# Loading-queue transfers for the block rows, late decays and h; roots on GpSimd; PSUM copies on ScalarE

## The chip, the cores and the metric

The kernel runs on one core of a Trainium2 chip. The metric is the device time of one execution in microseconds. The engines are named as the profile names them: PE is TensorE's matmul side, DVE is VectorE, ACT is ScalarE, POOL is GpSimd and SP is the engine whose queue issues the weight loads ("the loading queue").

## What is computed

One decoder block on 256 tokens of width 2048, in float32: a gated feed-forward layer, a mixer of two kinds of heads, a second feed-forward layer, gated per-layer embeddings and a final norm.

```python
def block(x, p, ...):                      # one block, SEQ = 256 tokens, D_MODEL = 2048, float32
    h = x
    h = h + 0.5 * swiglu(rmsnorm(h, ffn1_norm), w_gate, w_up, w_down)
    proj = rmsnorm(h, mix_norm) @ w_in
    g_qkv, g_gate, g_a, g_b, s_z, s_xbc, s_dt = jnp.split(proj, IN_SPLITS, axis=-1)
    o_gdn = gdn_mixer(g_qkv, g_gate, g_a, g_b, ...)       # 8 gated delta heads of 128
    o_ssm = ssd_mixer(s_z, s_xbc, s_dt, ...)              # 16 state-space heads of 64, 2 groups
    h = h + jnp.concatenate([o_gdn, o_ssm], axis=-1) @ w_out
    h = h + 0.5 * swiglu(rmsnorm(h, ffn2_norm), ...)
    gate = jax.nn.sigmoid(rmsnorm(h, ple_norm) @ ple_w_gate)
    h = h + gate * rmsnorm(p @ ple_w_proj, ple_post_norm)
    return rmsnorm(h, final_norm)

def gdn_mixer(qkv, gate, a, bl, conv_w, a_log, dt_bias, norm_w):
    qkv = jax.nn.silu(causal_depthwise_conv(qkv, conv_w))
    q, k, v = jnp.split(qkv, 3, axis=-1)                  # per head:
    q = l2norm(q) * 128 ** -0.5                           # x * rsqrt(sum(x * x) + EPS)
    k = l2norm(k)
    beta = jax.nn.sigmoid(bl)
    g = -jnp.exp(a_log) * jax.nn.softplus(a + dt_bias)
    o = gated_delta_rule_chunked(q, k, v, g, beta)        # a triangular solve per head and chunk
    return rmsnorm(o, norm_w) * jax.nn.silu(gate)
```

The state-space heads (`ssd_mixer`) are built alike: a causal convolution, decays from exponentials of cumulated sums, products per chunk and a state that is passed on.

## The kernel before

The work runs in stages. The positions are those of the profiled execution. The first feed-forward layer takes 0 to 764 us, the mixer 764 to 1156, the output projection `wout` 1156 to 1260, the second feed-forward layer 1260 to 2012, and the embeddings with the final norm the rest.

**Weights.** Tiles `raw` of 1 MB (128 x 2048) are loaded by SP (`load`, L108 to L112) into three buffers. Each is split in two pieces of 1024 columns: ScalarE casts the piece to a rounded format, `hi` (L119), and VectorE subtracts to get the rest, `lo` (L120); four buffers of each exist. In the mixer `single` (L136 to L150) multiplies a tile: for each of 16 blocks of 128 columns three matmuls, L146, L147 and L148, 48 in a tile and 24 in a piece. These are called weight matmuls below. A `lo` split needs the buffer that an earlier piece leaves when its last matmul is done.

**The mixer.** The projection by `w_in` goes on tile after tile, and the small work of the heads is interleaved with it. `delta_rule(i)` projects q, k and v of two delta heads (a pair, four of them) and starts the generator `gdn_pair`; `state_space(i)` does so for four state-space heads (a quad, four of them) with `ssd_quad`. A generator runs one piece further at each `tick()` of the weight loop, so its code order is tied to the weight loop. The scheduler then orders each engine's instructions on a simulated timeline and by priority, and each engine runs its list strictly in order.

The steps of a pair, with their lines:

1. `kk` (L578): products of k with k and q in a PSUM bank. L583 to L591 form `LA`, the decayed triangular blocks, and `ss`, the sums of squares.
2. `rs` (L602): the root `1/sqrt` of eight sums by `rsq` (L208 to L218), 11 VectorE steps: two integer steps for a first guess and three Newton steps of three. `irk` (L603) and `rq` (L605) follow from it.
3. Four small DMAs on GpSimd's queue write the 32-wide diagonal blocks of `LA` to DRAM as `blkl` (L612), and one reads them back as `Lb` (L614), each repeated over partitions, 512 KB. `Z` is preset to the unit blocks (L618), `Y` to zero (L621).
4. `xv` (L629) and `kd` (L636): ScalarE scales the transposed v and k.
5. The elimination: 31 columns of two VectorE steps each, `tb` (L645) and `Z` (L647), which invert the diagonal blocks.
6. `Z` goes to DRAM as `blky` (L648) and comes back in four parts as `Y` (L653), all on GpSimd's queue. VectorE transposes `Y` into `oT` (L656).
7. Two levels of small products, `ip`, `ix` and `iy` (L667), extend the inverse from blocks of 32 to 128.
8. The chain over the two chunks: `y0` (PSUM copy L703), `st` (copy to `S`, L707), `o0`, `ks` and `qs` (L711 to L716), `y1` (copy L719), `o1` (L722).
9. The output norm: squares on ScalarE (L727), `rq2` (L729 to L731), the root `ro` (L732) and its product with `rq` (L733), the scaling of `o` on ScalarE (L735), a transpose on TensorE, `ot` (L740), and a copy to `oT` (L741).

**Quads and decays.** The rows of cumulated decays lie in DRAM; `spread` (L427) reads them back onto all partitions into the space of `hT`, whose content is parked in DRAM as `hold` and read back at the end of the mixer (L873). `decay` adds a mask on GpSimd (L435) and takes exponentials on ScalarE (L439); `er` (L451) holds further ones. `late_decay` (L474) does this for quads 2 and 3 after the space is free. In `ssd_quad` two products of 128 x 512 on VectorE multiply the decays by `CB` (L802).

**Other roots.** `stats` (L220 to L239) uses the same `rsq` for the norms between stages; `finalrow` belongs to the final one.

The functions that the diff touches:

## Time and profile before

| what | us |
|---|---|
| median of 3 runs | 2114.48 |
| lowest and highest of them | 2114.13, 2115.96 |
| the profiled execution, its own time | 2113.53 |
| its span, first to last instruction | 2111.7 |
| PE busy in the span | 2069.7 |
| DVE busy | 1385.1 |
| ACT busy | 1030.4 |
| POOL busy | 130.8 |
| mean granted TensorE clock | 0.991 of full |

PE is busy 98% of the span. The view of stages gives the busy time of each engine between two positions, so a pause of PE is the length of the stretch less its busy time. The timelines list single instructions; in square brackets stands how long the engine had been idle before, and whose end released it. An `x4` in a row joins four instructions of one kind.

### The profile page before, as it was taken

What the parts mean: (1) busy time and instruction counts of PE and PEld (TensorE: products, weight loads), DVE (VectorE), ACT (ScalarE), POOL (GpSimd) and SP (SyncE); (2) the same over time, 40 slices, a digit from 0 to 9 for tenths busy, and PEclk for the clock granted to TensorE, in tenths of its full rate; (3) what the DMA queues carried; (4) which work ended last, traced back from release to release, by engine and by line L of the source; (5) the groups of instructions that cost most, each with busy time, mean ns of one, the idle gap of its engine ahead of it and who ended that gap; (6) DMA issues with size and microseconds to landing.
All of it is one profiled execution on the core that took longest, in us unless ns stands there. A gap on an engine that the chain in (4) does not pass through costs nothing.

```text
span 2111.7 us, 31624 instructions
## 1 busy us (share of the span) xinstructions
PE 2069.7 (98%) x12880; PEld 1848.4 (88%) x12880; DVE 1385.1 (66%) x2251; ACT 1030.4 (49%) x1529; POOL 130.8 (6%) x139
## 2 busy tenths in 40 slices
PE   8999999999999999999799999999999999999997
PEld 7888888888888899998798998888888888888886
DVE  7665555556556768989787667665555555556685
ACT  6444444444444556644344546544444444445553
POOL 2000000000000113001120011000000000000010
PEclk9999999999999999999899999999999999999998
DMA  7555455655545665553433545555456555545652
GB/s 252 192 184 183 171 180 190 213 180 187 192 165 188 208 209 187 195 208 124 144 133 140 184 163 198 193 187 182 165 189 206 196 181 184 195 157 185 207 189 100
DMA packets 63937, 384.58 MB, mean 182 GB/s; under 512 B 7584, under 2 KB 8864, under 8 KB 30640
## 3 DMA queue, kind: packets, MB, share of 16 engines
q1 hardware_dynamic: 59904, 372.04, 51.1%
q0 software_dynamic: 3888, 10.52, 1.8%
q8 instruction: 101, 1.65, 0.3%
q14 instruction: 44, 0.36, 0.1%
HBM read 377.78 MB, written 4.75 MB: 181 GB/s over the span
## 4 chain that ended last, share of the span: by engine, by line
PE 96%; DVE 2%; DMA 1%; issue 0%; ACT 0%; SPq 0%; POOL 0%; DVEq 0%; POOLq 0%
PE mm L131 49%; PE mm L129 24%; PE mm L147 6%; PE mm L148 6%; PE mm L146 6%; PE mm L133 1%; DVE lo L120 0%; DMA hT<-in_xT 0%; PE ip L667 0%; PE pj L131 0%; DMA blky<-Z 0%; PE py L814 0%; PE iy L667 0%; PE kk L578 0%; DVE pp L972 0%
## 5 line engine op out<-in xcount | busy, mean ns | idle before, releaser
L120 DVE TENSOR_TENSOR lo<-raw,hi 128x1024 fp32r<-128x1024 f32 (+1 forms) x774 | 858.6, 1117 | 487.3 <-ACT hi L119 486.5
L131 PE MATMUL mm<-xs,hi 128*128 128x512 f32 x3088 | 1079.2, 398 | 1.9 <-ACT hi L119 1.9
L119 ACT CAST hi<-raw 128x1024 fp32r<-128x1024 f32 (+1 forms) x774 | 744.5, 962 | 626.6 <-PE mm L131 374.9
L129 PE MATMUL mm<-xs,lo 128*128 128x256 f32 x2895 | 813.8, 281 | 3.4 <-DVE lo L120 3.4
L131 PEld LDWEIGHTS mm<-xs,hi 128*128 128x128 f32 x3088 | 568.8, 188 | 127.6 <-ACT hi L119 2.7
L129 PEld LDWEIGHTS mm<-xs,lo 128*128 128x128 f32 x2895 | 547.4, 189 | 13.4 <-DVE lo L120 5.0
L131 PE MATMUL mm<-hid,hi 128*128 128x512 f32 x1408 | 492.5, 397 | 0.0
L129 PE MATMUL mm<-hid,lo 128*128 128x256 f32 x1344 | 377.8, 281 | 0.0
L131 PEld LDWEIGHTS mm<-hid,hi 128*128 128x128 f32 x1408 | 260.2, 188 | 59.1
L129 PEld LDWEIGHTS mm<-hid,lo 128*128 128x128 f32 x1344 | 253.3, 188 | 3.0
L148 PE MATMUL mm<-xs,lo 128*128 128x256 f32 x816 | 232.9, 285 | 1.4 <-DVE lo L120 1.4
L146 PE MATMUL mm<-xs,hi 128*128 128x256 f32 x816 | 233.1, 286 | 0.0
L147 PE MATMUL mm<-xs,hi 128*128 128x256 f32 x816 | 232.4, 285 | 0.0
L148 PEld LDWEIGHTS mm<-xs,lo 128*128 128x128 f32 x816 | 156.5, 192 | 1.9 <-DVE lo L120 1.8
L146 PEld LDWEIGHTS mm<-xs,hi 128*128 128x128 f32 x816 | 156.7, 192 | 0.6 <-DVE cin L364 0.4
L147 PEld LDWEIGHTS mm<-xs,hi 128*128 128x128 f32 x816 | 156.6, 192 | 0.4 <-issue 0.2
L169 ACT COPY t<-mm 128x256 f32<-128x256 f32 x167 | 62.2, 373 | 160.1 <-PE mm L131 159.1
L170 DVE TENSOR_TENSOR t<-t,mm 128x256 f32<-128x256 f32 x167 | 69.8, 419 | 85.6 <-ACT t L169 85.5
L206 POOL TENSOR_TENSOR acc<-acc,sq 128x512 f32<-128x512 f32 x43 | 64.9, 1509 | 956.4 <-ACT sq L205 956.4
L169 ACT COPY s<-mm 128x256 f32<-128x256 f32 x88 | 32.7, 372 | 149.9 <-PE mm L131 149.9
L170 DVE TENSOR_TENSOR s<-s,mm 128x256 f32<-128x256 f32 x88 | 37.1, 421 | 74.2 <-ACT s L169 74.2
L146 PE MATMUL mm<-osp,hi 128*128 128x256 f32 x256 | 72.6, 284 | 1.2 <-ACT osp L196 1.2
(305 smaller groups left out, 1432.3 us busy)
## 6 DMA issues: line engine op xcount, KB each, us to landing
raw<-in_wgu SPq DMA_DIRECT2D x173, 1024.0 KB, 4.8
raw<-in_wd SPq DMA_DIRECT2D x128, 704.0 KB, 4.1
raw<-in_win SPq DMA_DIRECT2D x52, 1024.0 KB, 4.8
raw<-in_wout SPq DMA_DIRECT2D x16, 1024.0 KB, 4.8
raw<-in_wple SPq DMA_DIRECT2D x16, 1024.0 KB, 4.8
first<-in_wgu SPq DMA_DIRECT2D x12, 256.0 KB, 7.2
hold<-hT POOLq DMA_DIRECT2D x4, 512.0 KB, 3.9
hT<-rows POOLq DMA_DIRECT2D x4, 512.0 KB, 9.6
```

Of the source, the lines that this page charges most:

```text
L119: act.copy(hi, src)
L120: dve.tensor_tensor(out=lo, in0=src, in1=hi.bitcast(F32), op=ALU.subtract)
L129: pe.matmul(ps[:, 0, :], lo[:, w, :], act_in[:, k, 0, :], start=False, stop=False, skip_group_check=True)
L131: pe.matmul(ps, hi[:, w, :], act_in[:, k], start=start, stop=stop, skip_group_check=True)
L133: pe.matmul(ps[:, 0, :], lo[:, w, :], act_in[:, k, 0, :], start=False, stop=False, skip_group_check=True)
L146: pe.matmul(ps[:, 0, :], hi[:, i, :], act_in[:, k, 0, :], start=k == ks[0], stop=False)
L147: pe.matmul(ps[:, 0, :], hi[:, i, :], act_in[:, k, 1, :], start=False, stop=False)
L148: pe.matmul(ps[:, 0, :], lo[:, i, :], act_in[:, k, 0, :], start=False, stop=k == ks[-1])
L169: act.copy(out, ps[:, 0, :])
L170: dve.tensor_tensor(out=out, in0=out, in1=ps[:, 1, :], op=ALU.add)
L206: pool.tensor_tensor(out=acc, in0=acc, in1=sq, op=ALU.add)
```

## The change

- `rsq` takes its first value from GpSimd's power function and makes one Newton step of three VectorE steps after it. `stats` uses it.
- `rsq_aside` is new: the same wholly on GpSimd, the power and four steps. `rs` and `ro` use it. `irk`, `rq`, `rq2` and the product of `ro` and `rq` move from VectorE to GpSimd. A constant tile `mhalf` holds the exponent.
- The transfers `Lb`, the rows of `late_decay` and the reload of `hold` are issued by SP rather than GpSimd.
- The preset of `Z` moves from GpSimd to VectorE, and behind the four yields ahead of the elimination.
- The PSUM copies `y0`, `S` and `y1` move from VectorE to ScalarE, the products with `CB` from VectorE to GpSimd.

A line of the new kernel is that of before less 1 up to `rsq`, and plus 11 from about L219 on.

```diff
@@ -9,7 +9,6 @@
 
 F32 = mybir.dt.float32
 F32R = mybir.dt.float32r
-I32 = mybir.dt.int32
 AF = mybir.ActivationFunctionType
 ALU = mybir.AluOpType
 PSUM = bass.MemoryType.PSUM
@@ -208,14 +207,26 @@
     def rsq(m, n, name):
 
         y = small.tile([P, n], F32, tag=f"rsq{n}", name=name)
+        pool.tensor_tensor(out=y, in0=m, in1=mhalf[:, :n], op=ALU.pow)
         t = small.tile([P, n], F32, tag=f"rsqt{n}", name=name + "t")
-        dve.tensor_scalar(t.bitcast(I32), m.bitcast(I32), 1, None, op0=ALU.logical_shift_right)
-        dve.tensor_scalar(y.bitcast(I32), t.bitcast(I32), -1.0, float(0x5F3759DF), op0=ALU.mult, op1=ALU.add)
-        for _ in range(3):
-            dve.tensor_tensor(out=t, in0=y, in1=y, op=ALU.mult)
-            dve.scalar_tensor_tensor(out=t, in0=t, scalar=-0.5, in1=m, op0=ALU.mult, op1=ALU.mult)
-            dve.scalar_tensor_tensor(out=y, in0=t, scalar=1.5, in1=y, op0=ALU.add, op1=ALU.mult)
+        dve.tensor_tensor(out=t, in0=y, in1=y, op=ALU.mult)
+        dve.scalar_tensor_tensor(out=t, in0=t, scalar=-0.5, in1=m, op0=ALU.mult, op1=ALU.mult)
+        dve.scalar_tensor_tensor(out=y, in0=t, scalar=1.5, in1=y, op0=ALU.add, op1=ALU.mult)
         return y
+
+    def rsq_aside(m, n, name):
+
+        y = small.tile([P, n], F32, tag=f"rsq{n}", name=name)
+        pool.tensor_tensor(out=y, in0=m, in1=mhalf[:, :n], op=ALU.pow)
+        t = small.tile([P, n], F32, tag=f"rsqt{n}", name=name + "t")
+        pool.tensor_tensor(out=t, in0=y, in1=y, op=ALU.mult)
+        pool.tensor_tensor(out=t, in0=t, in1=m, op=ALU.mult)
+        pool.tensor_scalar(t, t, -0.5, 1.5, op0=ALU.mult, op1=ALU.add)
+        pool.tensor_tensor(out=y, in0=t, in1=y, op=ALU.mult)
+        return y
+
+    mhalf = cp.tile([P, 16], F32, name="mhalf")
+    pool.memset(mhalf, -0.5)
 
     def stats(squares, width, name, use, wait=2):
 
@@ -424,9 +435,9 @@
 
         ers = {}
 
-        def spread(d, src):
-
-            nc.gpsimd.dma_start(d, src.unsqueeze(0).to_broadcast([P, *src.shape]))
+        def spread(d, src, queue=nc.gpsimd):
+
+            queue.dma_start(d, src.unsqueeze(0).to_broadcast([P, *src.shape]))
 
         def decay(d, h0, n):
 
@@ -472,7 +483,7 @@
                 yield from quad_decay(i)
 
         def late_decay(i):
-            spread(quad_dec(i), rows[:, 8 + 4 * i:12 + 4 * i, :])
+            spread(quad_dec(i), rows[:, 8 + 4 * i:12 + 4 * i, :], nc.sync)
             for _ in range(3):
                 yield
             yield from quad_decay(i)
@@ -598,11 +609,11 @@
             for m, (c, hh) in enumerate(mats):
                 pe.matmul(ps[:, m:m + 1], sq[:, hh, tok[c]], ones[:, 0:1], start=True, stop=True)
             dve.tensor_scalar(ss[:, 4:8], ps[:, 0:4], EPS, None, op0=ALU.add)
-            rs = rsq(ss, 8, "rs")
+            rs = rsq_aside(ss, 8, "rs")
             irk = g2.tile([P, 4], F32, tag="irk", name="irk")
-            dve.tensor_tensor(out=irk, in0=ss[:, 0:4], in1=rs[:, 0:4], op=ALU.mult)
+            pool.tensor_tensor(out=irk, in0=ss[:, 0:4], in1=rs[:, 0:4], op=ALU.mult)
             rq = g2.tile([P, 4], F32, tag="rq", name="rq")
-            dve.tensor_scalar(rq, rs[:, 4:8], float(P) ** -0.5, None, op0=ALU.mult)
+            pool.tensor_scalar(rq, rs[:, 4:8], float(P) ** -0.5, None, op0=ALU.mult)
             yield
 
 
@@ -611,11 +622,10 @@
             for q, p in enumerate(parts):
                 nc.gpsimd.dma_start(bl.rearrange("(m b) j i -> b j m i", m=4)[q], LT[p, :, p])
             Lb = g2.tile([P, BS, BS], F32, tag="Lb", name="Lb", bufs=1)
-            nc.gpsimd.dma_start(Lb.rearrange("p j i -> p (j i)"),
+            nc.sync.dma_start(Lb.rearrange("p j i -> p (j i)"),
                               bl.rearrange("q j i -> q (j i)").unsqueeze(1).to_broadcast([P // NG, NG, BS * BS]))
             Z = g2.tile([P, CG, BS], F32, tag="Z", name="Z", bufs=1)
             tb = g2.tile([P, CG * BS], F32, tag="tb", name="tb", bufs=1)
-            pool.tensor_copy(Z, unit)
 
             Y = g2.tile([P, 4, P], F32, tag="Y", name="Y")
             pool.memset(Y, 0.0)
@@ -636,6 +646,7 @@
                 act.mul(kd[:, hh, :], ps[:, hh * P:(hh + 1) * P], kdw[:, hh:hh + 1])
             for _ in range(4):
                 yield
+            dve.tensor_copy(Z, unit)
 
             for j in range(BS - 1):
                 if j % STEP == 0:
@@ -700,11 +711,11 @@
             o = g2.tile([P, 4, P], F32, tag="o", name="o", bufs=1)
             y0, y1 = xv[:, 0:2, :], xv[:, 2:4, :]
             ps = two([Y[:, hh, :] for hh in range(2)], y0, "y0")
-            dve.tensor_copy(y0, ps)
+            act.copy(y0, ps)
             yield
             yield
             ps = two([kd[:, hh, :] for hh in range(2)], y0, "st")
-            dve.tensor_copy(S, ps)
+            act.copy(S, ps)
             ps = two([LA[:, hh, 1, :] for hh in range(2)], y0, "o0")
             act.copy(o[:, 0:2, :], ps)
             yield
@@ -716,7 +727,7 @@
                 act.mul(qs[:, hh, :], pq[:, hh, :], egc[:, h0 + hh:h0 + hh + 1])
             yield
             ps = two([Y[:, 2 + hh, :] for hh in range(2)], y1, "y1")
-            dve.tensor_copy(y1, ps)
+            act.copy(y1, ps)
             yield
             ps = two([LA[:, 2 + hh, 1, :] for hh in range(2)], y1, "o1")
             dve.tensor_tensor(out=o[:, 2:4, :], in0=ps, in1=qs, op=ALU.add)
@@ -726,11 +737,11 @@
             for m in range(4):
                 act.activation(qs[:, m % 2, :], o[:, m, :], AF.Square, accum_out=so[:, m:m + 1])
             rq2 = g2.tile([P, 4], F32, tag="rq2", name="rq2")
-            dve.scalar_tensor_tensor(out=rq2, in0=rq, scalar=1.0 / P, in1=rq, op0=ALU.mult, op1=ALU.mult)
-            dve.tensor_tensor(out=rq2, in0=rq2, in1=so, op=ALU.mult)
-            dve.tensor_scalar(rq2, rq2, EPS, None, op0=ALU.add)
-            ro = rsq(rq2, 4, "ro")
-            dve.tensor_tensor(out=ro, in0=ro, in1=rq, op=ALU.mult)
+            pool.tensor_tensor(out=rq2, in0=rq, in1=rq, op=ALU.mult)
+            pool.tensor_tensor(out=rq2, in0=rq2, in1=so, op=ALU.mult)
+            pool.tensor_scalar(rq2, rq2, 1.0 / P, EPS, op0=ALU.mult, op1=ALU.add)
+            ro = rsq_aside(rq2, 4, "ro")
+            pool.tensor_tensor(out=ro, in0=ro, in1=rq, op=ALU.mult)
             for m in range(4):
                 act.mul(o[:, m, :], o[:, m, :], ro[:, m:m + 1])
             for _ in range(4):
@@ -799,7 +810,7 @@
             dve.tensor_tensor(out=xe, in0=xd[:, 0],
                               in1=dte[:, 8 + h0:12 + h0].unsqueeze(2).to_broadcast([P, 4, 64]), op=ALU.mult)
             for c in range(2):
-                dve.tensor_tensor(out=ds[c], in0=ds[c], in1=over(CB[:, 2 * c + g, :], 4), op=ALU.mult)
+                pool.tensor_tensor(out=ds[c], in0=ds[c], in1=over(CB[:, 2 * c + g, :], 4), op=ALU.mult)
             yield
             yield
             ps = mx_bank("ss0")
@@ -870,7 +881,7 @@
 
 
         for k in range(0, KD, 4):
-            nc.gpsimd.dma_start(hT[:, k:k + 4, :], hold[:, k:k + 4, :])
+            nc.sync.dma_start(hT[:, k:k + 4, :], hold[:, k:k + 4, :])
         for i in range(3):
             gate(i, oT[:, 2 * i:2 * i + 2, :])
         drain(gdn + norms)
```

The order of the instructions moves with it at three places.

VectorE at the end of pair 2's elimination, before (`tb` and `Z` are the elimination's steps, `lo` a weight split; the last `Z` of the pair is the 128x4 step, and the 128x124 step begins the next pair's):

```order
L645 TENSOR_TENSOR tb<-Lb,Z 128x4
L605 TENSOR_SCALAR rq<-rs 128x4
L647 TENSOR_TENSOR Z<-Z,tb 128x4
L729 SCALAR_TENSOR_TENSOR rq_11037<-rq 128x4
L802 TENSOR_TENSOR hT<-hT,CB 128x512
L645 TENSOR_TENSOR tb<-Lb,Z 128x124
L647 TENSOR_TENSOR Z<-Z,tb 128x4x31
L645 TENSOR_TENSOR tb<-Lb,Z 128x120
L647 TENSOR_TENSOR Z<-Z,tb 128x4x30
L645 TENSOR_TENSOR tb<-Lb,Z 128x116
L647 TENSOR_TENSOR Z<-Z,tb 128x4x29
L656 STREAM_TRANSPOSE oT<-Y 128x512
```

The same place in the new order:

```order
L656 TENSOR_TENSOR tb<-Lb,Z 128x4
L658 TENSOR_TENSOR Z<-Z,tb 128x4
L119 TENSOR_TENSOR lo<-raw,hi 128x1024 x3
L649 COPY Z<-cont 128x128
L656 TENSOR_TENSOR tb<-Lb,Z 128x124
L658 TENSOR_TENSOR Z<-Z,tb 128x4x31
...
L119 TENSOR_TENSOR lo<-raw,hi 128x1024
L658 TENSOR_TENSOR Z<-Z,tb 128x4x29
L656 TENSOR_TENSOR tb<-Lb,Z 128x112
...
L119 TENSOR_TENSOR lo<-raw,hi 128x1024
L658 TENSOR_TENSOR Z<-Z,tb 128x4x27
L667 STREAM_TRANSPOSE oT<-Y 128x512
```

Before, no split stands between the last `Z` and the transpose that ends the pair's way through DRAM; now five do, counting the `x3` row as three.

GpSimd at the same place, before (`blky` and `Y` are the way of pair 2 through DRAM, `Lb` and `blkl` belong to pair 3):

```order
L612 DMA blkl_6789<-LA 32x4x32 x4
L429 DMA hT<-rows 128x2x512
L614 DMA Lb<-blkl_6789 128x1x1024
L648 DMA blky_6788<-Z 128x128
L435 TENSOR_TENSOR hT<-hT,cont 128x512
L653 DMA Y<-blky_6788 32x4x32 x3
L618 COPY Z<-cont 128x128
L653 DMA Y<-blky_6788 32x4x32
```

The same place in the new order (L220 to L225 and L740 to L744 are roots, `rs` of pair 3 and `ro` of pair 1, L813 the product with `CB`):

```order
L223 TENSOR_TENSOR rst<-rst,ss 128x8
L224 TENSOR_SCALAR rot<-rot 128x4
L659 DMA blky_6776<-Z 128x128
L224 TENSOR_SCALAR rst<-rst 128x8
L225 TENSOR_TENSOR ro<-rot,ro 128x4
L813 TENSOR_TENSOR hT<-hT,CB 128x512
L225 TENSOR_TENSOR rs<-rst,rs 128x8
L744 TENSOR_TENSOR ro<-ro,rq 128x4
L614 TENSOR_TENSOR irk<-ss,rs 128x4
L616 TENSOR_SCALAR rq<-rs 128x4
L740 TENSOR_TENSOR rq_10969<-rq 128x4
L664 DMA Y<-blky_6776 32x4x32 x4
```

`Lb` stands no longer ahead of `blky`; between `blky` and the reads of `Y` stand one product with `CB` and seven small steps.

TensorE from pair 0's `o0` to the end of the cluster, before (`y_8737` is `y1`, `o_8815` is `o1`; `kk`, `ss`, `vt` and `kt` are pair 2's, `xt` is quad 0's):

```order
L696 MATMUL o_8604<-xv,LA 128x128 x2
L696 MATMUL ks<-S,KQ 128x128 x2
L696 MATMUL qs<-S,KQ 128x128
L578 MATMUL kk<-KQ 128x256 x2
L696 MATMUL qs<-S,KQ 128x128
L578 MATMUL kk<-KQ 128x256 x2
L599 MATMUL ss<-ones,ksq 128x1 x4
L696 MATMUL y_8737<-xv,Y 128x128 x2
L626 MATMUL vt<-cont,V 128x128 x4
L696 MATMUL o_8815<-xv,LA 128x128 x2
L633 MATMUL kt<-cont,KQ 128x128 x2
L793 MATMUL xt<-cont,XS 128x128 x4
```

The new order, around `ks`:

```order
L145 MATMUL mm<-xs,hi 128x256
L707 MATMUL ks<-S,KQ 128x128 x2
L707 MATMUL qs<-S,KQ 128x128
L589 MATMUL kk<-KQ 128x256 x2
L707 MATMUL qs<-S,KQ 128x128
L589 MATMUL kk<-KQ 128x256 x2
L146 MATMUL mm<-xs,hi 128x256
```

The cluster is taken apart. The weight matmuls (`mm`) that stand between one step and the next, counted in the order:

| from, to | before | after |
|---|---|---|
| pair 0 `y0`, `st` | 0 | 24 |
| pair 0 `o0`, `ks` | 0 | 20 |
| pair 2 `kk`, `ss` | 0 | 14 |
| pair 0 `y1`, pair 2 `vt` | 0 | 24 |
| pair 2 `vt`, pair 0 `o1` | 0 | 3 |
| pair 0 `o1`, pair 2 `kt` | 0 | 8 |
| pair 2 `kt`, quad 0 `xt` | 0 | 5 |
| quad 1 `xt`, pair 1 `ot` | 24 | 104 |
| pair 1 `ot`, pair 2 `ip` | 0 | 16 |
| pair 2 `ip` of the first level, `ip` of the second | 0 | 0 |
| pair 3 `o1`, `ot` | 50 | 66 |
| pair 3 `ot`, first of `wout` | 0 | 50 |

## Rows read from the trace of the kernel before

**Rows 1.** Busy us (instructions) by engine, then TensorE clock; the mixer.

```profile
764.00:1156.00 392.00, 369.24 (x2984) 358.64 (x2983) 327.09 (x898) 190.42 (x340) 62.28 (x82) 0.97 0.50 167
```

**Rows 2.** The same view, 20-us stretches of the mixer.

```profile
840.00:860.00 20.00, 18.58 (x153) 18.17 (x152) 20.00 (x31) 16.34 (x36) 5.00 (x6) 1.00 0.72 240
...
960.00:980.00 20.00, 16.89 (x116) 14.68 (x115) 18.55 (x83) 8.23 (x22) 3.51 (x7) 0.91 0.29 105
...
1020.00:1040.00 20.00, 17.75 (x145) 17.34 (x143) 17.91 (x89) 7.68 (x17) 3.45 (x6) 1.00 0.42 140
1040.00:1060.00 20.00, 8.08 (x43) 6.80 (x44) 9.30 (x34) 4.42 (x14) 5.44 (x9) 0.57 0.34 96
...
1140.00:1160.00 20.00, 15.95 (x114) 14.79 (x113) 15.45 (x34) 11.93 (x26) 0.00 (x0) 0.91 0.45 159
```

**Rows 3.** Timeline, TensorE: start, us, engine line op names [idle before <-releaser].

```profile
1040.53 1.21 PE L740 MATMUL ot<-cont,o 128*128 128x128 f32 x4 [2.79 <-ACT o L735]
1053.12 0.69 PE L667 MATMUL ip<-oT,LA 128*128 128x64 f32 x2 [11.39 <-DVE oT L656]
...
1062.08 0.36 PE L146 MATMUL mm<-xs,hi 128*128 128x256 f32 x1
...
1152.48 1.21 PE L740 MATMUL ot<-cont,o 128*128 128x128 f32 x4 [2.79 <-ACT o L735]
```

**Rows 4.** Timeline, VectorE, at 825 and from 1040.

```profile
825.90 1.23 DVE L215 TENSOR_TENSOR rst<-rs 128x8 f32<-128x8 f32 x1
...
1040.23 0.17 DVE L647 TENSOR_TENSOR Z<-Z,tb 128x4 f32<-128x4 f32 x1
...
1044.32 0.69 DVE L802 TENSOR_TENSOR hT<-hT,CB 128x512 f32<-128x512 f32 x1 [3.85 <-ACT hT L439]
...
1052.36 0.70 DVE L656 STREAM_TRANSPOSE oT<-Y 128x512 f32<-128x512 f32 x1
```

**Rows 5.** Timeline, GpSimd, at 825, 979 and from 1040.

```profile
825.81 1.29 POOL L435 TENSOR_TENSOR hT<-hT,cont 128x512 f32<-128x512 f32 x1 [1.85 <-DMA hT<-rows]
...
979.15 0.57 POOL L648 DMA_DIRECT2D blky<-Z  x1 [2.07 <-DVE u L539]
...
981.45 1.65 POOL L653 DMA_DIRECT2D Y<-blky  x3 [1.14 <-DMA blky<-Z]
...
1040.49 0.57 POOL L614 DMA_DIRECT2D Lb<-blkl  x1 [4.42 <-DVE rq L729]
1041.05 0.58 POOL L648 DMA_DIRECT2D blky<-Z  x1
...
1048.57 1.68 POOL L653 DMA_DIRECT2D Y<-blky  x3 [5.64 <-DMA blky<-Z]
```

**Rows 6.** Timeline, VectorE, from pair 3's last squares.

```profile
1146.18 0.16 DVE L730 TENSOR_TENSOR rq<-rq,so 128x4 f32<-128x4 f32 x1
...
1151.83 0.16 DVE L733 TENSOR_TENSOR ro<-ro,rq 128x4 f32<-128x4 f32 x1
```

**Rows 7.** DMA issues of w_in tiles: count, KB each, median us to landing.

```profile
raw<-in_win SPq DMA_DIRECT2D x52, 1024.0 KB, 4.8
```

**Rows 8.** Groups by line: count, busy us, mean ns, idle before; weight splits.

```profile
L120 DVE TENSOR_TENSOR lo<-raw,hi 128x1024 fp32r<-128x1024 f32 (+1 forms) x774 | 858.6, 1117 | 487.3 <-ACT hi L119 486.5
...
L119 ACT CAST hi<-raw 128x1024 fp32r<-128x1024 f32 (+1 forms) x774 | 744.5, 962 | 626.6 <-PE mm L131 374.9
```

**Rows 9.** Timeline, all engines, the final norm.

```profile
2099.53 0.17 DVE L212 TENSOR_SCALAR finalt<-finalm 128x2 int32<-128x2 int32 x1
...
2101.72 1.22 PE L238 MATMUL finalrow<-cont,final 128*128 128x128 f32 x4 [2.42 <-DVE final L217]
```

**Rows 10.** Timeline, ScalarE, around 838.

```profile
837.60 0.84 ACT L451 ACTIVATE er<-hT 64x256 f32<-64x256 f32 x2 [2.03 <-DMA hT<-rows]
...
839.95 2.44 ACT L439 ACTIVATE hT<-hT,ngc 128x128 f32<-128x128 f32 x8
```

## The prediction

> **What bounds the kernel now.** I read first the busy time of each engine by stage. In the feed-forward stages TensorE never pauses, and nothing in the change touches them; in the mixer (764 to 1156) it is busy 369.24 of 392 us, so 22.76 us of pauses lie there, while VectorE has 327.09 of the 392 [rows 1]. Next the 20-us stretches of the mixer: five of them hold all the pauses, 1.42 us (A, 840 to 860), 3.11 (B, 960 to 980), 2.25 and 11.92 (C, 1020 to 1060) and 4.05 (D, 1140 to 1160), and in B, C and D the granted clock sinks to 0.91, 0.57 and 0.91 [rows 2]. Busy time at the lower of the two levels (1.2 in place of 2.4 GHz) does half the work, so a stretch of 20 us at mean clock c has lost 20 x (1 - c) us to it as an upper bound: 1.8 in B, 8.6 in C, 1.8 in D. In C most of the 8.6 is the pause itself, which would have done nothing anyway. Worked out directly: the weight matmuls before C end at 1040.53 - 2.79 = 1037.74, those after it begin at 1062.08 [rows 3], 24.3 us later. Of these 14.2 are pauses; the other 10.1 are the small matmuls of pair and quad, most of them at the lower clock, which I count at two thirds, 6.8 us. So C costs about 17.5 us. The whole to win is 1.4 + 4.9 + 17.5 + 5.9, about 30 us.
>
> Then what TensorE waits for. At C it waits 2.79 us at `ot` for ScalarE's `o`, and 11.39 us at `ip` for VectorE's transpose `oT` [rows 3]. The way back goes over three engines: the last elimination step `Z` is at 1040.23 [rows 4]; GpSimd then first issues the next pair's `Lb` (0.57), then `blky`, and the reads `Y` start only at 1048.57, after 5.64 us on `blky`; the transpose is at 1052.36 [rows 4, 5]. Where no `Lb` (512 KB) was issued ahead, from `blky` to the first `Y` read it is 979.15 to 981.45, 2.3 us, against 7.5 us here [rows 5]. At D it waits 2.79 us at `ot` [rows 3], for the root of pair 3: VectorE takes from 1146.18 to 1151.83 for steps of 0.2 us each, since weight splits of 1.2 us lie between them [rows 6].
>
> **The change, part by part.**
> *`Lb` to the loading queue.* In the new order no `Lb` stands before `blky` on GpSimd. At C this takes away 0.57 us of issue and up to 7.5 - 2.3 = 5.2 us of transfer that shared the way. The loading queue gets three kinds of waits in return: 4 `Lb`, 2 `late_decay` rows, 4 `hold` reloads. Behind each stand weight loads of 1 MB, 4.8 us to landing [rows 7]; a tile lasts TensorE 48 x 0.12 = 5.7 us and three buffers exist, so a load may be late by about 2 x 5.7 - 4.8 = 6.6 us before it shows. The producers of these transfers precede in the order the split that frees the next buffer, so I take 0, bounds 0 to 4 us.
>
> *VectorE is relieved.* A root was 11 steps; `rs` and `ro` go away whole, with `irk`, `rq`, the three `rq2` steps and the last product: per pair 11 + 2 + 11 + 4 = 28 steps of 0.08 to 0.2 us, some 4 us; with it two products by `CB` of 0.69 per quad [rows 4], and three copies of 256 elements per pair, 0.4 each by the same row. Added is the `Z` copy of 128 elements, under 0.3. Over four pairs that is 16 + 5.5 + 5 - 1.2, about 25 of 327 us. It pays only where VectorE is late. The order shows it at C: the last `Z` of pair 2 now has five weight splits between it and the transpose, before none. A split serves 24 matmuls, 2.9 us, so the elimination is finished about 5 x 2.9 = 14 us earlier against TensorE's row; the chain of 12.1 us from last `Z` to transpose [rows 4] then starts before TensorE arrives, and shortened by 5 it is hidden. What is late next: the transpose still stands behind the split of a piece whose buffer comes free with the last matmul before `ip`, so cast 0.96, split 1.12 [rows 8] and transpose 0.70 [rows 4] remain, 2.8 us. With that wait, the small waits of a cluster without weight matmuls in between, and some time at the lower clock, C keeps 4.5 to 14.5 of its 17.5 us. I take a **gain of 8** (3 to 13), nearer the middle since the order leaves the cluster of small products as it was.
>
> *B.* Before, all of pair 0's second half and pair 1's start stand without a weight matmul between; in the new order 3 to 24 weight matmuls stand between most of these steps, which covers waits of 0.5 to 1.7 us. Of 4.9 lost I take back **4** (0 to 4.5).
>
> *D.* The new order has 66 weight matmuls (7.9 us) between the last `o1` and `ot`, before 50, and 50 more (6 us) behind `ot`. The root is now nine GpSimd steps. One dependent step costs VectorE 0.2 us [rows 9]; taken for GpSimd too, with the squares and the scaling ahead and behind (some 2.5 us) it is 4.5 us, under 7.9. **Gain 5.5** (2 to 6.5).
>
> *A.* On ScalarE the new order sets all four `er` steps, the last of which wait for a transfer (2.03 us [rows 10]), ahead of one weight cast, and 12 exponentials ahead of the next, where 8 stood in a row (2.44 us [rows 10], so 3.7 for 12). A piece lasts TensorE 2.9 us, and VectorE is full here (20.00 of 20 [rows 2]). I take **-3** (-4 to +1).
>
> *The root's price.* No row has the power function. From below: a VectorE step of the same size, 0.17 us; from above: a GpSimd product of 64 times the elements, 1.29 us [rows 5, 9]. I take 0.3, since the tiles have 2 to 8 elements per partition. The final norm's root stood wholly on the path: 11 steps from 2099.53 in a wait of 2.42 us [rows 9]; now one power and three steps, 0.3 + 0.6 and a hop between engines: **gain 1** (-0.2 to +1.3).
>
> *New waits.* ScalarE now waits for GpSimd at `xv` and at `o`, and queued behind these are weight casts. GpSimd also gets the `CB` products, 1.29 us or more where VectorE took 0.69 [rows 4, 5]. While GpSimd does such a product VectorE stalls: its step at 825.90, of a size that takes 0.17 at 2099.53, took 1.23 us beside a GpSimd product from 825.81 to 827.10 [rows 4, 5, 9]. So eight products of 0.69 that leave VectorE may hold it up to 8 x 1.29 all the same; I take **-1.5** (-4 to 0). The Trainium skill (GPSIMD Engine Reference, section 1, Specifications) says that GpSimd shares its SBUF interface with VectorE, with contention for VectorE instructions with two SBUF inputs; the row agrees, and it speaks against moving the products: by it VectorE gains nothing from them, and the time would be the first rival's rather than the forecast.
>
> **Sum.** 8 + 4 + 5.5 - 3 + 1 - 1.5 = 14. The profiled execution took 2113.53 us, so 2099.5; the median of the runs shown, 2114.48, is 0.95 above it, so **2100.5** forecast for the median.
>
> **The rivals.**
> *GpSimd holds VectorE up.* The lock just read hits mostly the elimination, steps with two SBUF inputs; eight products and the twelve mask additions of the decays stand around pairs 1 to 3. Then the last `Z` of pair 2 comes some 5, not 14 us earlier and C gives 1, B 2, D 5.5, A -3, the rest -0.5: a gain of 5, **2109.5**. Against it: a product locks 1.3 us once, and VectorE has 2.09 us of pauses in 1020 to 1040 and 10.70 in 1040 to 1060 [rows 2] to take it up.
>
> *The power function is long (slower than before).* One mechanism: GpSimd runs in order, each root gates a ScalarE step, weight casts stand behind that and TensorE behind these. Eight roots of the pairs and the final one: 9 x (X - 0.3) us over the forecast, with X the price of one. It decides from X = 0.3 + 14/9, 1.9 us; at 3 us the time is 2100.5 + 24, **2125**. For it: no row has the function. Against: 64 times as many elements take 1.29.
>
> *The loading queue blocks.* If an `Lb` or a reload waits longer than the 6.6 us of cover, every later load moves; four such of 4 us, less the gain: **2116**.
>
> *More is closed.* If C keeps only its floor and A does not worsen: C 13, B 4.5, D 6, A 0, and 1 - 1.5 as above, 23 in all: **2091.5**.
>
> **How the numbers follow.** Forecast (2094 to 2107) 0.60; VectorE held up (2107 to 2113) 0.17; long power function 0.12; loading queue 0.04; more closed 0.07. About 0.2%, 4.2 us, is what a measurement can tell from no change here. Faster: 0.60 + 0.07 + half of the second, 0.08: 0.75. Slower: the long function, 0.11, the queue's worse half, 0.02, and 0.02 from the second: 0.15. The rest, 0.10, is the same. The range 2088 to 2113 takes in the first two cases and most of the last, and leaves out the slower ones, about 0.18.
>
> **What would show it.** In the new profile: at pair 2's `ip` a wait of some 3 us in place of 11.39; no wait at the last `ot`; from `blky` to the first `Y` read 2 to 3 us in every pair; the stretch at A worse by 1 to 4 us of pauses; a power step of 0.2 to 0.6 us on GpSimd. A power step over 1.5 us, TensorE waits on weight casts released by GpSimd, or a loading queue with pauses over 6 us would prove me wrong; so would an elimination whose steps grow to 1.2 us beside GpSimd's products.

## The result and the profile after

The changed kernel takes 2085.02 us (median of 4 runs, 2080.95 to 2085.97) against 2114.87 before (4 runs); the ratio is 0.9855, with a 95% interval of 0.9838 to 0.9872. That is 29.9 us less, where 14 were forecast and the range ended at 2088. The profiled execution has a span of 2083.2 us, before 2111.7.

The stages and the mixer's stretches that still hold pauses, after (stretch, length, then busy us and instructions of PE, its weight loads, VectorE, ScalarE and GpSimd, then the granted clock):

```profile
764.00:1130.00 366.00, 354.58 (x2985) 346.80 (x2985) 306.61 (x738) 192.46 (x351) 101.06 (x142) 0.98 0.51 175
1130.00:1156.00 26.00, 26.00 (x222) 26.00 (x222) 20.30 (x26) 14.60 (x19) 2.02 (x2) 1.00 0.56 194
```

```profile
820.00:840.00 20.00, 18.71 (x161) 18.19 (x159) 12.87 (x18) 15.97 (x41) 16.63 (x20) 1.00 0.50 175
840.00:860.00 20.00, 19.53 (x163) 19.12 (x161) 19.68 (x41) 13.70 (x24) 0.00 (x0) 1.00 0.79 255
...
880.00:900.00 20.00, 19.14 (x167) 18.94 (x166) 19.86 (x39) 8.07 (x10) 5.80 (x5) 1.00 0.42 152
...
920.00:940.00 20.00, 17.07 (x135) 16.67 (x136) 18.80 (x50) 6.96 (x9) 0.00 (x0) 0.91 0.47 160
...
1020.00:1040.00 20.00, 14.13 (x104) 13.31 (x103) 11.69 (x28) 8.22 (x18) 7.87 (x16) 0.77 0.60 196
...
1120.00:1140.00 20.00, 20.00 (x174) 20.00 (x173) 15.00 (x21) 12.44 (x20) 2.06 (x5) 1.00 0.48 164
```

Beside [rows 1] the mixer ends some 26 us earlier. Beside [rows 2] the pauses sum to 11.4 us, before 22.8. C has 5.87 us in place of 14.2, D none. The pauses in 820 to 840 (1.29 us), 880 to 900 (0.86) and 920 to 940 (2.93) are new. VectorE has 306.61 us of work in the mixer, before 327.09, so it was relieved by 20 us (25 were worked out); GpSimd has 101.06, before 62.28.

TensorE at C, after (timeline, as [rows 3]):

```profile
1034.09 0.69 PE L678 MATMUL ip<-oT,LA 128*128 128x64 f32 x2 [5.87 <-DVE oT L667]
```

The wait of 11.39 at `ip` is 5.87 now, and the 2.79 at `ot` ahead of it are gone. What released it, on VectorE (first fence, answering to [rows 4]) and on GpSimd (second, answering to [rows 5]):

```profile
1017.15 0.17 DVE L658 TENSOR_TENSOR Z<-Z,tb 128x4 f32<-128x4 f32 x1
...
1022.50 2.63 DVE L119 TENSOR_TENSOR lo<-raw,hi 128x1024 fp32r<-128x1024 f32 x2 [3.44 <-ACT hi L118]
...
1033.32 0.71 DVE L667 STREAM_TRANSPOSE oT<-Y 128x512 f32<-128x512 f32 x1 [0.62 <-DMA Y<-blky]
```

```profile
1018.65 1.56 POOL L446 TENSOR_TENSOR hT<-hT,cont 128x512 f32<-128x512 f32 x1 [2.01 <-DMA hT<-rows]
...
1020.47 0.63 POOL L659 DMA_DIRECT2D blky<-Z  x1
...
1021.60 1.30 POOL L813 TENSOR_TENSOR hT<-hT,CB 128x512 f32<-128x512 f32 x1
1022.86 1.18 POOL L225 TENSOR_TENSOR rs<-rst,rs 128x8 f32<-128x8 f32 x1
1024.01 1.18 POOL L744 TENSOR_TENSOR ro<-ro,rq 128x4 f32<-128x4 f32 x1
...
1025.95 2.22 POOL L664 DMA_DIRECT2D Y<-blky  x4
```

The last `Z` of pair 2 comes at 1017.15, before at 1040.23. The way from there to the transpose, 12.1 us before, has not become shorter but longer, 16.2 us: `blky` stands 3.3 us behind the last `Z` in GpSimd's queue, behind a mask addition, and the reads `Y` stand 5.5 us behind `blky` (7.5 before), behind a product by `CB` and the small steps of two roots. The gain at `ip` comes from the earlier start alone: the last `Z` lay 2.5 us behind TensorE's last weight matmul ahead of the cluster before, and lies 11.1 us ahead of it now.

The root at the final norm and the one of pair 3 (GpSimd, then TensorE at the final norm, answering to [rows 6, 9]):

```profile
1117.07 0.20 POOL L741 TENSOR_TENSOR rq<-rq,so 128x4 f32<-128x4 f32 x1 [13.92 <-ACT qs L738]
...
1117.63 1.01 POOL L220 TENSOR_TENSOR ro<-rq,mhalf 128x4 f32<-128x4 f32 x1
...
1121.48 0.20 POOL L744 TENSOR_TENSOR ro<-ro,rq 128x4 f32<-128x4 f32 x1
```

```profile
2071.60 0.71 POOL L210 TENSOR_TENSOR final<-finalm,mhalf 128x2 f32<-128x2 f32 x1 [7.53 <-DVE finalm L243]
...
2072.94 1.22 PE L249 MATMUL finalrow<-cont,final 128*128 128x128 f32 x4 [1.62 <-DVE final L214]
```

Pair 3's root takes 4.6 us on GpSimd from first to last step, before 5.8 on VectorE [rows 6]; `ot` follows without a wait. At the end the wait is 1.62 in place of 2.42.

### The profile page after: what moved, and what is told of

Its sections match the earlier page's. It is cut to its first block, busy times and chain, and to the rows that moved or that the text cites. A ratio compares the mean times of both kernels' runs of the same rounds, so it can differ in the third digit from the quotient of the medians.

```text
span 2083.2 us, 31507 instructions
## 1 busy us (share of the span) xinstructions
PE 2055.1 (99%) x12880; PEld 1837.5 (88%) x12880; DVE 1361.0 (65%) x2059; ACT 1034.6 (50%) x1541; POOL 173.5 (8%) x206
## 4 chain that ended last, share of the span: by engine, by line
PE 92%; DMA 2%; issue 2%; DVE 2%; POOL 1%; ACT 1%; SPq 0%; POOLq 0%; DVEq 0%; ACTq 0%
PE mm L130 50%; PE mm L128 24%; PE mm L145 4%; PE mm L147 4%; PE mm L146 4%; PE mm L132 1%; DMA hT<-rows 1%; DVE lo L119 1%; ACT hT L450 0%; PE ip L678 0%; DMA hT<-in_xT 0%; PE pj L130 0%; POOL hT L813 0%; PE py L825 0%; DMA blky<-Z 0%
## 5 line engine op out<-in xcount | busy, mean ns | idle before, releaser
L145 PE MATMUL mm<-xs,hi 128*128 128x256 f32 x816 | 230.7, 283 | 0.5 <-ACT hi L118 0.5
L146 PE MATMUL mm<-xs,hi 128*128 128x256 f32 x816 | 228.9, 280 | 0.0
L147 PE MATMUL mm<-osp,lo 128*128 128x256 f32 x256 | 71.7, 281 | 0.0
```

The costliest lines, as they stand in the source:

```text
L145: pe.matmul(ps[:, 0, :], hi[:, i, :], act_in[:, k, 0, :], start=k == ks[0], stop=False)
L146: pe.matmul(ps[:, 0, :], hi[:, i, :], act_in[:, k, 1, :], start=False, stop=False)
L147: pe.matmul(ps[:, 0, :], lo[:, i, :], act_in[:, k, 0, :], start=False, stop=k == ks[-1])
```

## The experiments

There are two questions: which part of the change gave the gain, and whether the new order of the instructions gave it at all. The second arises because the constant tile `mhalf` has 64 bytes per partition and lies ahead of the weight buffers `raw`, `hi` and `lo`, so these lie 64 bytes further on, while the activations `xs` stay. In the mixer of the changed kernel the weight matmuls run closer together than before. Three kernels with the same order of instructions on every engine, at the same place (TensorE's timeline; the start is the first column): the change (tile of 64 bytes), the tile at 128 bytes, the tile at 256 bytes.

```profile
904.86 0.28 PE L145 MATMUL mm<-xs,hi 128*128 128x256 f32 x1
904.97 0.28 PE L146 MATMUL mm<-xs,hi 128*128 128x256 f32 x1
905.09 0.28 PE L147 MATMUL mm<-xs,lo 128*128 128x256 f32 x1
905.20 0.28 PE L145 MATMUL mm<-xs,hi 128*128 128x256 f32 x1
```

```profile
904.90 0.28 PE L145 MATMUL mm<-xs,hi 128*128 128x256 f32 x1
905.02 0.28 PE L146 MATMUL mm<-xs,hi 128*128 128x256 f32 x1
905.14 0.28 PE L147 MATMUL mm<-xs,lo 128*128 128x256 f32 x1
905.25 0.28 PE L145 MATMUL mm<-xs,hi 128*128 128x256 f32 x1
```

```profile
904.96 0.28 PE L145 MATMUL mm<-xs,hi 128*128 128x256 f32 x1
905.08 0.28 PE L146 MATMUL mm<-xs,hi 128*128 128x256 f32 x1
905.20 0.28 PE L147 MATMUL mm<-xs,lo 128*128 128x256 f32 x1
905.32 0.28 PE L145 MATMUL mm<-xs,hi 128*128 128x256 f32 x1
```

Three steps take 0.34, 0.35 and 0.36 us. Over the mixer the mean distance of neighbouring weight matmuls is 0.114, 0.119 and 0.120 us, and 0.120 before the change.

All runs, with the ratio to the kernel before and its interval. The last column is the time from the first w_in matmul to the first matmul behind `wout` in the profiled execution, that is mixer and output projection together; it was 472.8 us before. The runs are from several chips, so the ratios are to be compared and not the medians. The last column comes from one execution of each kernel, and those of one kernel lie 2 to 9 us apart (a_copy: 2088.11 to 2097.53), so differences of 1 to 4 us in it are no more than hints.

| kernel | median us | ratio (95%) | mixer and wout us |
|---|---|---|---|
| the change | 2085.02 | 0.9855 (0.9838 to 0.9872) | 445.7 |
| b_pad64 | 2108.05 | 0.9971 (0.9959 to 0.9982) | 469.5 |
| b_pad32 | 2111.55 | 0.9990 (0.9981 to 0.9999) | 473.1 |
| a_pad0 | 2082.04 | 0.9841 (0.9818 to 0.9864) | 450.4 |
| a_pad128 | 2080.91 | 0.9849 (0.9833 to 0.9866) | 447.3 |
| a_pad192 | 2083.40 | 0.9845 (0.9824 to 0.9866) | 453.4 |
| a_pad256 | 2089.08 | 0.9880 (0.9863 to 0.9898) | 449.6 |
| a_root | 2096.80 | 0.9908 (0.9893 to 0.9923) | 456.6 |
| a_short | 2097.41 | 0.9914 (0.9899 to 0.9929) | 456.6 |
| a_copy | 2088.74 | 0.9881 (0.9860 to 0.9901) | 449.5 |
| a_cb | 2088.51 | 0.9870 (0.9855 to 0.9884) | 447.7 |
| a_queue | 2085.68 | 0.9866 (0.9852 to 0.9881) | 446.7 |
| b_root | 2094.25 | 0.9900 (0.9884 to 0.9915) | 457.5 |
| b_root0 | 2095.91 | 0.9904 (0.9887 to 0.9922) | 464.3 |
| a_xs3 | 2085.48 | 0.9854 (0.9838 to 0.9871) | 445.1 |
| a_xs3p128 | 2083.32 | 0.9844 (0.9827 to 0.9861) | 453.7 |

### Place or order

**b_pad64, b_pad32** add only an unused tile to the kernel before, ahead of the weight buffers:

```diff
+    pad = cp.tile([P, 16], F32, name="pad")     # b_pad32: 8
```

> The kernel before with an unused tile of 64 bytes per partition ahead of the weight buffers; the order of the instructions is the same on every engine, the weight buffers move by 64 bytes against the activations. Theory 1, the distance of the addresses sets the pace: the w_in matmuls go from 0.120 to 0.113 us apart, 2400 x 0.006 = 14 us, so 2100. Theory 2, the pace comes from the new order or from which engines work beside TensorE: 2114.

> The kernel before with 32 bytes in place of 64. Theory 1: the pace of the w_in matmuls is that of a distance of 32 modulo 64, as in the output projection, where it is 0.118: 2400 x 0.0015 = 4 us less, 2110 (2100 to 2112). Theory 2: 2114.

Each place has a pace of its own: 0.115 us in the mixer for 64 bytes, 0.118 for 32. The time of b_pad64, 2108.05, lies between the two theories. With 64 the w_in matmuls alone would give some 10 us, and the weight matmuls of mixer and wout do take 7.1 us less, yet mixer and wout fall by 3.3 only: the pauses are 1.0 us longer, and the small matmuls take 2.8 us more, since C stands at the lower clock for longer in this execution. Its two stretches at C, to be compared with the clock in [rows 2], 1.00 and 0.57:

```profile
1020.00:1040.00 20.00, 13.86 (x107) 12.83 (x105) 14.78 (x80) 10.15 (x27) 5.35 (x8) 0.88 0.61 203
1040.00:1060.00 20.00, 12.68 (x64) 12.05 (x65) 12.94 (x40) 3.11 (x8) 4.28 (x7) 0.50 0.18 45
```

So the place counts, at a fraction of what its pace would give, and does not explain the 30 us.

**a_pad0, a_pad128, a_pad192, a_pad256** are the change with the constant tile moved behind the weight buffers, or made larger:

```diff
-    mhalf = cp.tile([P, 16], F32, name="mhalf")
+    mhalf = small.tile([P, 16], F32, tag="mhalf", name="mhalf", bufs=1)   # a_pad0
+    mhalf = cp.tile([P, 32], F32, name="mhalf")                           # a_pad128; 48, 64
```

> The changed kernel with its constant tile at 128 in place of 64 bytes per partition, order the same. Theory 1, the addresses: the w_in matmuls go back to 0.120 us apart and the time to 2085 + 14 = 2099. Theory 2, the new order or the moved work sets the pace: 2085.

> The changed kernel with the constant tile at 256 bytes, order the same. If the pace of the matmuls hangs on the weight buffers' place modulo 128 or 256 bytes, it repeats the place of 128 or of none: 2081 to 2086, feed-forward sums of 349.9 or 352.9 ns for a hi and a lo matmul. If on larger steps, a pace seen nowhere yet: 2075 to 2095.

> The changed kernel with its constant tile behind the weight buffers, which so stand at the addresses of the kernel before; order the same as the change. If the place modulo 256 bytes sets the pace, as the tile of 256 bytes suggests: 2089 (2087 to 2091), of the 30 us some 25 from the order and 4 to 5 from the place. If the order alone made the gain: 2085.

> The changed kernel with the constant tile at 192 bytes, a place modulo 256 not seen so far. If 64 and 192 mirror each other: 2085 with 0.113 us in the mixer. If it takes after 128: 2081 with feed-forward sums of 349.9 ns. If it is as none: 2089.

The expectation for a_pad128 was wrong: the mixer's pace did go back, nearly to that of before, but mixer and wout grew by 1.6 us only, and the feed-forward stages became faster, by 3.8 us in the first one. a_pad256 shows in all stages the distances of the kernel before (its groups of 241, 236, 233 and 232 ns for a 512-column matmul and 120 ns in the mixer come back with nearly the same shares), so a move by 256 bytes is as none; its time, 2089.08, lies above the range that was expected of it. It is the cleanest measure of the order alone: 0.9880, mixer and wout 23.2 us shorter. a_pad0 has the weight buffers of before, too, but moves all tiles behind them by 64 bytes, and its time, 2082.04, speaks against the first of its expectations: mixer and wout are 22.4 us shorter, and 9.0 us more lie outside them. Of these, 7.2 are the `hid` products (the second ones of the two feed-forward stages), which take 244.7 us a stage in place of 248.3. So the order gives 22 to 23 us in mixer and wout at the old place of the weights, and the rest of each ratio is place. The ratios of the five places spread over 0.4%, with intervals that overlap; a_pad192, with a pace of 0.118 us in the mixer, fits none of its three theories by that, and lies with the lower ratios.

### Which part

**a_root** puts `rs`, `ro`, `irk`, `rq`, `rq2` and the last product back on VectorE in the old form; **a_short** puts them on VectorE in the new short form, a power on GpSimd and three steps:

```diff
-            rs = rsq_aside(ss, 8, "rs")
+            rs = rsq(ss, 8, "rs")            # a_root: the 11 old steps, a_short: power + 3
-            pool.tensor_tensor(out=irk, in0=ss[:, 0:4], in1=rs[:, 0:4], op=ALU.mult)
+            dve.tensor_tensor(out=irk, in0=ss[:, 0:4], in1=rs[:, 0:4], op=ALU.mult)
```

> The changed kernel with the roots rs and ro, irk, rq, rq2 and their product back on VectorE in the old 11-step form. Its order puts the last ot of pair 3 directly ahead of the output projection again, with 44 weight matmuls behind o1. If the roots on VectorE made C and D late: D's 7 us come back and part of C's, 2094 to 2102. If the copies, the CB products or the queue did it: 2084 to 2088.

> The changed kernel with rs and ro as a power on GpSimd and three steps on VectorE, and irk, rq, rq2 and the product on VectorE. If the number of VectorE steps in the way counts (28 a pair before, 12 here, 0 in the change): a little under half of the 11 us of the full undoing, 2088 to 2091. If only a way clear of VectorE's queue counts: 2094 to 2097. If leaving VectorE was of no use and the short root did it: 2085.

Both give back the same sum, 11.0 us of mixer and wout, and both ratios are clear of the change's. But the sums are made up differently. At D, a_root loses 8.1 us against the change and a_short nothing. VectorE's timeline of a_root shows why D is late, for pair 3's `ro`:

```profile
1128.80 0.17 DVE L222 TENSOR_SCALAR rot<-rq 128x4 int32<-128x4 int32 x1
...
1129.82 1.23 DVE L120 TENSOR_TENSOR lo<-raw,hi 128x1024 fp32r<-128x1024 f32 x1
...
1132.53 1.22 DVE L120 TENSOR_TENSOR lo<-raw,hi 128x1024 fp32r<-128x1024 f32 x1
...
1134.35 0.15 DVE L746 TENSOR_TENSOR ro<-ro,rq 128x4 f32<-128x4 f32 x1
```

The root takes 5.5 us, though its steps take 0.2 each: splits and evacuations stand in between. In a_short the same root takes 3.4 us (1123.25 to 1126.47), less than the change's 4.6, and 82 weight matmuls cover it. TensorE's waits from 1000 to 1145, a_root and then the change (last columns: total us, count, longest):

```profile
PE ot L753 <- ACT o L748: 8.1, 2, 4.6
PE ip L680 <- DVE oT L669: 4.6, 1, 4.6
PE ss L819 <- DVE xe L812: 2.3, 1, 2.3
```

```profile
PE ip L678 <- DVE oT L667: 5.9, 1, 5.9
```

In a_root both waits at `ot` come back, at C and at D. In a_short neither does; it loses 13.9 us at C and is 2.9 us faster elsewhere. At C pair 2's elimination comes late (VectorE, then TensorE):

```profile
1030.02 0.17 DVE L658 TENSOR_TENSOR Z<-Z,tb 128x4 f32<-128x4 f32 x1
...
1042.48 0.71 DVE L667 STREAM_TRANSPOSE oT<-Y 128x512 f32<-128x512 f32 x1
```

```profile
1043.25 0.69 PE L678 MATMUL ip<-oT,LA 128*128 128x64 f32 x2 [16.59 <-DVE oT L667]
```

The last `Z` stands behind TensorE's last weight matmul (1025.94) again, and no split stands between it and the transpose, as before the change. So a short root on VectorE is enough at D and not at C, and that the two sums agree is chance. How much of the loss at C is the steps themselves and how much the order that the scheduler made with them, no run tells.

**a_copy, a_cb, a_queue** take back one of the other parts each:

```diff
-            act.copy(y0, ps)                                    # a_copy; S and y1 alike
+            dve.tensor_copy(y0, ps)
-                pool.tensor_tensor(out=ds[c], in0=ds[c], ...)   # a_cb
+                dve.tensor_tensor(out=ds[c], in0=ds[c], ...)
-            nc.sync.dma_start(Lb...)                            # a_queue; late_decay, hold alike
+            nc.gpsimd.dma_start(Lb...)
```

> The changed kernel with the copies of y0, S and y1 back on VectorE. If each copy sat in a chain that TensorE waited for: 2087 to 2090. If they were covered: 2084 to 2086.

> The changed kernel with the products by CB back on VectorE. If GpSimd's products lock VectorE and gain nothing: 2083 to 2086, the same or a little less. If VectorE's relief by 5.5 us counts: 2087 to 2091.

> The changed kernel with Lb, the late decay rows and the reload of h back on GpSimd's queue. If the way blky to Y is what the queue move shortens, the wait at pair 2's ip grows by 3 to 6 us and the time is 2088 to 2092. If relief of VectorE alone did it, within 2 us of 2085.

By mixer and wout the copies are worth 3.8 us, the products 2.1 and the queue 1.0. The ratios of all three overlap that of the change, so for the copies and the products only the sign is likely, and for the queue not even that. The expectation that without the queue move the wait at pair 2's `ip` grows was wrong: it is 4.03 us in a_queue, but a wait of 5.02 us at the `ot` ahead of it is back. That GpSimd's products lock VectorE so that the move gains nothing has no support in a_cb; it isn't ruled out for single places. With the 11.0 us of the roots, the parts taken back singly come to 17.9 of 27.1 us. The preset of `Z` was not taken back in any run.

**b_root, b_root0** give the kernel before the new roots alone, with the constant tile ahead of or behind the weight buffers:

```diff
-            rs = rsq(ss, 8, "rs")
+            rs = rsq_aside(ss, 8, "rs")
```

> The kernel before with the new roots alone (power and small steps on GpSimd, the constant tile of 64 bytes among it, which by itself gave 0.9971). The order has 75 weight matmuls between pair 3's o1 and ot and 51 behind. If the roots work alone as they do in the company of the other moves, where taking them back cost 0.0053: 0.9971 - 0.0053 = 0.992, 2098. If they need the other moves: 2103 to 2108.

> The kernel before with the new roots alone and the weight buffers at their old addresses. If place and order add up: 0.990 / 0.9971 = 0.993, 2100. If the place was the part that counted there: 2108 to 2112.

Both have a ratio of 0.990, better than expected, but not for the same reason, and it isn't the roots' worth alone. Of b_root0's gain 9.0 us lie outside mixer and wout, most of it by the place of `hid` as in a_pad0, and 8.5 in them; b_root has 15.3 in them, with the place of 64 bytes, which brought b_pad64 3.3. So the new roots alone are worth some 8.5 to 12 us, in accord with the 11.0 of a_root: under half of the whole. D's wait is gone in b_root0 as well, C's isn't (6.05 us at `ot`, 10.55 at `ip`).

### What is late next

**a_xs3** gives the state-space inputs `XS` a third buffer (and puts `gct` into the place of `th`, for room); **a_xs3p128** is that with the tile at 128 bytes:

```diff
-            XS = m2.tile([P, 2, T], F32, tag="XS", name="XS")
+            XS = m2.tile([P, 2, T], F32, tag="XS", name="XS", bufs=3)
```

> The changed kernel with a third XS buffer (and gct in the place of th). Theory: at C no weight matmul can stand inside the cluster, since the next one needs a PSUM bank whose evacuation zt waits for the one u buffer, this for XS of quad 3, and this for quad 1, which is in the cluster. With a third XS the order has 55 weight matmuls more ahead of pair 2's ip and the cluster taken apart: 5.9 us of pauses and some 5 us at half clock go, 2074 to 2080. Rival, the pauses at C come from the way through DRAM of pair 2: then the wait stays and the time is 2083 to 2087.

> The changed kernel with the third XS buffer and the constant tile at 128 bytes. Each alone gave 2085 and 2081 on chips on which the change itself gives 2085. If the two are apart from each other: 2081. If the third XS pays once the weight matmuls are a little slower in the mixer: 2076 to 2080.

The stretches of a_xs3 at C and at the end:

```profile
1020.00:1040.00 20.00, 19.43 (x172) 18.94 (x171) 15.42 (x36) 10.02 (x20) 5.23 (x9) 1.00 0.60 201
1040.00:1060.00 20.00, 19.36 (x172) 18.35 (x170) 19.45 (x55) 9.77 (x17) 4.66 (x4) 1.00 0.40 129
1100.00:1120.00 20.00, 18.23 (x161) 18.04 (x159) 12.77 (x24) 10.65 (x22) 3.00 (x5) 1.00 0.45 159
1120.00:1140.00 20.00, 16.26 (x104) 15.37 (x105) 11.90 (x18) 10.56 (x19) 2.27 (x6) 0.74 0.25 81
```

The waits at C are gone: pair 2's `ip` waits 0.57 us in place of 5.87. This bears out the cause that was named: without a third `XS` no weight matmul could stand inside the cluster (the links over `u` and the PSUM bank are read from the code). At the 6200th weight matmul this kernel is 15.3 us ahead of the change, but that isn't all gain: half of the 100 small matmuls of the stretch at C, 7.6 us of its time, now stand outside it, nearly all behind. At the end of wout the lead is 0.6 us. What was put off accounts for part of the loss; the rest is new waits, where pair 3's `ot` waits 4.2 us and the output projection right behind it 1.2, and the lower clock there (0.74 in 1120 to 1140). So the time, 2085.48, lies where the rival had put it, though the wait that the rival wanted to stay is gone: the expectation left out the end. a_pad128 (ratio 0.9849) and a_pad0 (0.9841) lie below the change by a little, with intervals that overlap its own; a_xs3p128 adds nothing to that, and its interval can't tell its two expectations apart.

## Why the prediction was wrong

The direction and the places B, C and D were right, the size was not: 14 us were forecast and 29.9 came. No single step explains it. The steps that failed are sizes: the charge at A (off by 3.9 us), C (2.6), D (1.7), the charge for new waits (1.1) and B (0.9) were all too cautious, 10.2 us together, and the shift of the weight buffers, 3.9, had no term. By stretches between the same weight matmuls (counted from the start), before, in a_pad256 (order alone) and in the change:

| stretch | before | a_pad256 | change | gain of order | forecast |
|---|---|---|---|---|---|
| A, from the first w_in matmul to the 5400th | 143.2 | 142.3 | 139.3 | 0.9 | -3 |
| B, to the 6100th | 115.8 | 110.9 | 111.2 | 4.9 | 4 |
| C, to the 6200th | 40.4 | 29.8 | 31.0 | 10.6 | 8 |
| to the 6700th | 74.8 | 75.2 | 72.8 | -0.4 | new waits, -1.5 |
| D, to the end of wout | 98.6 | 91.4 | 91.3 | 7.2 | 5.5 |
| sum | 472.8 | 449.6 | 445.7 | 23.2 | 13 |

Some half a microsecond of the gain of C and of that of D is only moved: four `xt` matmuls and the four `ot` of pair 3 stand behind the mark at the start of these stretches before and ahead of it after.

**A, the largest error (4 us).** The step charged 3 us for exponentials and `er` ahead of weight casts. The order came as read: 12 exponentials do stand between two casts, and `er` waits for its transfer. But A still gains 0.9 us at the old places, with pauses of 0.64 us in place of 1.42; in the change itself its pauses grow to 2.62 (1.29, 0.47 and 0.86 us), within what was said, and the faster pace outweighs them. So the charge put the length of ScalarE's steps down as lost, almost without cover. Which cover took them up, no run tells.

**New waits (1.1 us).** They were charged for weight casts queued behind ScalarE's waits for GpSimd. All waits of TensorE from 764 to 1160, after:

```profile
PE ip L678 <- DVE oT L667: 8.8, 2, 5.9
PE mm L147 <- DVE lo L119: 2.1, 2, 1.3
PE mm L145 <- ACT hi L118: 0.5, 1, 0.5
```

Only 0.5 us is released by a weight cast. New is the 2.9 us at pair 1's `ip`, the pause in 920 to 940, with a granted clock of 0.91 there; it is in the stretch of B, whose gain is 4.6 in the change and 4.9 at the old places, where this wait is 0.67.

**C (2.6 us).** The 14 us by which the last `Z` moves held (13.6). The argument that the way from there is shortened by 5 us, so that it is hidden, fell: `blky` to the first `Y` read became 2 us shorter only, and `blky` itself stood longer behind the last `Z`, both behind other work in GpSimd's queue, the roots and a product new among it, so that the whole way grew by 4.1. The floor that was named (2.8 us) isn't what ended the wait; the transpose waited 0.62 us for `Y`, the rest of 5.87 was earlier links of the same way. C was sized from the middle of a wide range; the rows gave no reason to keep any of the wait at `ot`, and this wait went whole.

**D (1.7 us).** The 66 matmuls cover the root, as forecast, but with luck. The 4.5 us of the forecast were for the whole way, squares and scaling included, and left 3.4 us to spare; the nine GpSimd steps alone took 4.6, the way from the end of `o1` (1115.16) to the start of the scaling (1121.71) 6.5, and the 66 matmuls 7.3, so less than 1 us was to spare. The whole loss, put at 5.9 from [rows 2], went, the lower clock (0.91 before, 1.00 after) with it; the other 1.2 us in the table are the four `ot` matmuls, which stand in the stretch ahead after.

**B** was within 0.9, the final norm within 0.2 (0.8 for 1).

**Places, 3.9 us in mixer and wout**, had no step at all. The prediction doesn't mention the constant tile, and says that nothing in the change touches the feed-forward stages; the tile moves the weight buffers of all stages. The 3.9 are what is left of a faster pace: between a_pad256 and the change the weight matmuls gain 9.6 us, the pauses grow from 6.8 to 11.4, and the small matmuls take 1.1 us more at the lower clock. b_pad64 shows a gain by place alone that is clear of noise (0.9971); the ratios of a_pad256 and the change overlap.

**The root's price** was wrong in its upper bound: the power takes 0.71 us for 2 elements per partition, 1.0 to 1.2 for 4 and 1.6 to 1.9 for 8, where 0.3 was taken and 1.29 set as the end; two of those of 2 elements take 1.70 and 1.75. Eight elements are dearer than 512 of a product: the bound by number of elements doesn't hold across operations. A power step over 1.5 us was named as a sign of being wrong and came, but the rival that hung on it, 9 x (X - 0.3) us over the forecast, did not: of TensorE's waits in the list above only 0.5 us are released by a weight cast, the last link of its path. The small steps of two roots do stand ahead of pair 2's `Y` reads at C, so the roots' length is part of the 5.87 us left there.

**The first rival**, VectorE held up by GpSimd, gave 2109.5; it fell with the measured time and the 20 us of relief, and the sign of a_cb agrees. **The loading queue** did stand still for longer than the 6 us that were named as a sign: up to 9.0 us for `blkl` ahead of `Lb`, 9.0 ahead of the late decays and 10.6 ahead of the reload of `hold`. But no weight cast of the mixer waited for its `raw`, so this cost nothing that the trace shows; that it gained anything isn't shown either (a_queue).

GpSimd is held up beside VectorE, too: its steps at 1022.86 and 1024.01 take 1.18 us beside the weight splits from 1022.50, and the second is of a kind that takes 0.20 at 1121.48. The Trainium skill (GPSIMD Engine Reference, section 1, Specifications) says that GpSimd shares its SBUF interfaces with VectorE, with contention where a VectorE instruction has two SBUF inputs, as a split has; this trace agrees. Such stalls lengthen a root on GpSimd.

## What to carry to other kernels

A chain of small dependent steps on a full in-order engine costs not its own microseconds but the large steps that are queued between its links. Moving the chain away whole helped at both places here; shortening it (a_short) helped at one and not at the other, so look at each place and not at the sum. Charge a loss only where a row shows the cover used up. When a wait is taken out of one cluster, ask what was only put off and which wait the later stage has in store: a_xs3 was 15.3 us ahead at one mark and 0.6 at the end. Before crediting an edit of the schedule, look whether it allocates anything: an unused tile of 64 bytes took 0.3% off by itself.
